# Attention stage of a hybrid layer: score tiles in a ring of three banks, q and k held twice, sample caches in the merge tile, attention written ahead of all projections

## The chip, the cores and the metric

One core of a Trainium2 chip runs the whole program in one launch. The time is device microseconds of that core. The kernel before took 1383.82, 1389.14 and 1391.13 us in three runs, so the median is 1389.14. The profile is of one more execution.

## The reference, cut to what matters

One layer of a streaming encoder runs on 512 prompt tokens and 32 sample tokens (the sample has a cache of 512 past keys and values). An input projection makes q, k and v of eight heads, the operands of a recurrent branch (RWKV-7) and two gates. Branch A is differential attention, the stage that changes: two softmax maps per head, subtracted with a learned factor, times v, then a norm per head.

```python
def diff_attend(q, k, v, lam, mask):          # q, k: 8 heads x 2 maps x 64; v: 8 heads x 128
    s = jnp.einsum('bqhcd,bkhcd->bchqk', q, k) * (DA_HEAD_DIM ** -0.5)
    if mask is not None:                      # the prompt: chunks of 64, block causal
        s = jnp.where(mask, s, -1e30)
    p = jax.nn.softmax(s, axis=-1)
    pd = p[:, 0] - lam * p[:, 1]
    return jnp.einsum('bhqk,bkhd->bqhd', pd, v)
...
x = x + (g_da * (o @ w_o_da) + g_rw * (o_rw @ w_o_rw)) @ w_out
x = x + ffn(rmsnorm(x))                       # up-projection, convolution of width 3, down-projection
```

## The kernel before, in words

Activations are held transposed, features on the 128 partitions and 544 tokens on the free axis (512 prompt, 32 sample). A projection (`dense_g`, L222) makes 128 output features in two halves of 272 tokens. Weights arrive in blocks of 128 x 512, a 256 KB load on SyncE's queue each (`load_w`, L212); ScalarE casts the high part `wh`, VectorE or GpSimd subtracts to get the low part `wl`, and a block gives 4 x 3 matmuls (`wh*xh`, `wh*xl`, `wl*xh`) for each half, 24 in all. One group of 1024 input features has two blocks, so 48 matmuls, into two tiles `psd` of PSUM, one for each half. Three `psd` banks exist. A half is evacuated when its last matmul is done.

The program has these stages: norm and recurrent branch with input projections among them; attention (L1091 to L1376), with what is left of the input projections ("fillers": v and gate tiles, written to DRAM by `fill_tile`) and the eight groups of `w_orw` among it; then the eight groups of `w_oda` (L1391), `w_out`, the up-projection, the down-projection and the last norm.

In the attention stage, `load_head` (L1252) fetches one head: v into `vt`; q and k into `raw`, split into `hi` (ScalarE) and `lo` (VectorE), and copied by small transfers into `Q`, `KH` and `KL`, so that both maps have all 128 partitions. Every one of these tiles has one buffer. `scores` (L1278) does a block of 128 queries: for each of the two maps a matmul with KH and one with KL into the tile `sc` (two banks, one buffer), a mask, a row maximum over both maps (`nm`, VectorE), two exponentials (`E`, ScalarE), and the difference `pd` (VectorE). `weighted` (L1308) transposes `pd`, copies it to `pdt`, and multiplies with v into `po`; after the fourth block `attend_norm` (L1113) makes the norm, and `finish_head` transposes back and writes `dh` and `dl` by `put_z`. `attend_sample` (L1177) does the same for four heads of the sample at once, against the caches in the tile `kc` (one buffer, first keys, then values).

The order around the change comes from two things. The program text is written by small generators that `Flow.run` interleaves by estimated due times (`yield ...`), with dense work in between. Then a scheduler builds each engine's queue: of the instructions whose operands and buffers it estimates to be ready, it takes the one written first. Each engine runs its queue in that order and waits at an instruction whose operand is late. SyncE's queue carries nearly all loads, also in order.

Of the kernel before, what the change touches and what calls it, by code (L numbers as in the profile page):

```python
# [10 lines left out]
F32 = mybir.dt.float32  # L11
F32R = mybir.dt.float32r
# [14 lines left out]
SEQ = 512  # L27
# [134 lines left out]
def tile_hybrid_layer(  # L162
# [931 lines left out]
    ap = ph2.enter_context(tc.tile_pool(name="ap", bufs=1, reuse_waits="tile"))  # L1094
    pst = ph2.enter_context(tc.tile_pool(name="pst", bufs=2, space=PSUM))
# [17 lines left out]
    def attend_norm(po, rz0, n, name="on"):  # L1113

        ssq = ap.tile([128, 4], F32, name="ssq", bufs=2)
        on = ap.tile([128, n, 128], F32, name=name)
# [19 lines left out]
    mg = mp.tile([128, KT, TOK], F32, name="mg")  # L1136
# [7 lines left out]

    zs = new_hl()
    load_z(mp, z_d, *zs, G)
    under = list(range(KT))
    flow.mark("z", 14.0)

    def orw_g(i):  # L1150
        nc.sync.dma_start(out=mg[:, i, :], in_=t_d[8 + i])

        def ev(ps, c0, c1):
            V.scalar_tensor_tensor(out=mg[:, i, c0:c1], in0=mg[:, i, c0:c1], scalar=1.0, in1=ps,
                                   op0=ALU.add, op1=ALU.mult)
        yield from dense_g(w_orw[i], KT, *zs, ev, V if i + 40 in FV else G)

    def choose2():
        if fillers:
            return fillers.pop(0)()  # L1160
        return orw_g(under.pop(0)) if under and flow.done["z"] <= PE.now else None

    att_dense = Dense(choose2)
# [9 lines left out]
    def load_caches(g):  # L1173
        caches[g] = ap.tile([128, 4, PAST], F32, name="kc")
        nc.sync.dma_start(out=caches[g], in_=kcache[4 * g:4 * g + 4].rearrange("a p t -> p a t"))

    def attend_sample(g):  # L1177
# [6 lines left out]
        yield PE.now + 1.0  # L1184
        sc = pssc.tile([128, 2, 512], F32, name="sc")
        kc = caches[g]
        for e, hh in enumerate(hs):
            for m in range(2):
                PE.matmul(sc[32 * e:32 * e + 32, m, :], qks[m * 64:m * 64 + 64, 0, hh, :],
                          kc[m * 64:m * 64 + 64, e, :], start=True, stop=True,  # L1190
                          tile_position=(64 * m, 32 * e))
        vc = ap.tile([128, 4, PAST], F32, name="kc").rearrange("p a (b v) -> p a b v", v=128)
        nc.sync.dma_start(out=vc, in_=vcache[4 * g:4 * g + 4].rearrange("a p b v -> p a b v"))
# [8 lines left out]
        V.tensor_reduce(out=nm, in_=sc, axis=AX.X, op=ALU.max, negate=True)  # L1202
        for m in range(2):
            V.tensor_reduce(out=nm2[:, m:m + 1], in_=scn[m][:, 0:32], axis=AX.X, op=ALU.max, negate=True)
        V.tensor_tensor(out=nm, in0=nm, in1=nm2, op=ALU.min)
        E = ap.tile([128, 2, 512], F32, name="E", bufs=2)
        En = ap.tile([128, 2, 32], F32, name="En")
        Z4 = ap.tile([128, 2, 2], F32, name="Z4")
        for m in range(2):
            A.activation(out=E[:, m, 0:PAST], in_=sc[:, m, :], func=AF.Exp, bias=nm[:, m:m + 1], scale=1.0,  # L1210
                         accum_out=Z4[:, 0, m:m + 1])
            A.activation(out=En[:, m, :], in_=scn[m][:, 0:32], func=AF.Exp, bias=nm[:, m:m + 1], scale=1.0,
                         accum_out=Z4[:, 1, m:m + 1])
# [21 lines left out]
        yield PE.now + 1.5  # L1235
# [8 lines left out]
        on = attend_norm(po[:, 0:1, :], rz1[:, 0:1], 1, "son")  # L1244
        yield PE.now + 5.0
# [32 lines left out]
    def scores(i, Q, KH, KL, rz):  # L1278

        nk = 128 * (i + 1)  # L1280
        sc = pssc.tile([128, 2, 512], F32, name="sc")
        nm = ap.tile([128, 2], F32, name="nm", bufs=3)
        E = ap.tile([128, 2, 512], F32, name="E", bufs=2)
# [3 lines left out]
        n = max(nk, 256)  # L1287
        for m in range(2):
            PE.matmul(sc[:, m, 0:n], Q[:, m, qb], KH[:, m, 0:n], start=True, stop=False)
            PE.matmul(sc[:, m, 0:n], Q[:, m, qb], KL[:, m, 0:n], start=False, stop=True)  # L1290
        V.memset(sc[0:64, :, nk - 64:nk], -1e30)
        V.tensor_reduce(out=nm, in_=sc[:, :, 0:nk], axis=AX.X, op=ALU.max, negate=True)
        for m in range(2):
            A.activation(out=E[:, m, 0:nk], in_=sc[:, m, 0:nk], func=AF.Exp, bias=nm[:, m:m + 1], scale=1.0,  # L1294
                         accum_out=Z[:, m:m + 1])
# [4 lines left out]
        V.scalar_tensor_tensor(out=pd[:, 0:nk], in0=E[:, 1, 0:nk], scalar=Z[:, 2:3], in1=E[:, 0, 0:nk],  # L1300
# [3 lines left out]
    def attention():  # L1304
# [3 lines left out]
        def weighted(h, i, pd, at, vtok, rz):  # L1308

            yield at  # L1310
# [9 lines left out]
            yield t  # L1320
# [11 lines left out]
        def finish_head():  # L1332
            yield last["at"]
# [8 lines left out]
        yield PE.now + 9.0  # L1342
        for h in range(HEADS):
# [5 lines left out]
            for i in range(4):  # L1349
                yield sc_free  # L1350
# [12 lines left out]
    def samples():  # L1363
        for g, h in ((0, 1), (1, 4)):
# [11 lines left out]
    hscope.close()  # L1376

# [279 lines left out]
```

## Time and profile before

| what | value |
|---|---|
| median of 3 runs | 1389.14 us (1383.82 to 1391.13) |
| profiled execution, its own time | 1387.72 us |
| its span, first to last instruction | 1385.9 us |
| TensorE busy | 1273.7 us, 92% |
| VectorE, ScalarE, GpSimd busy | 63%, 42%, 17% |
| mean granted TensorE clock | 0.941 of full speed |
| DMA | 185.9 MB, mean 134 GB/s |

The span is cut into 40 slices on the page; each digit is a busy share in tenths. A timeline names an instruction by line, engine and tiles (`out<-in`), with the idle time before it and what ended that. A granted clock of 1.00 is 2.4 GHz and 0.50 is 1.2 GHz; a mean between them is a mix of both.

### The profile page before, as it was taken

How to read it: one execution, taken by the hardware profiler on the slowest of the kernel's cores; microseconds unless marked ns; L12 is line 12 of the kernel's file. 1: busy time of each engine (PE TensorE's matmuls, PEld its weight loads, DVE VectorE, ACT ScalarE, POOL GpSimd, SP SyncE). 2: the span in 40 equal slices, each digit the busy share in tenths (PEclk: the TensorE clock that was granted, in tenths of full speed). 3: DMA queues.
4: the chain of work that ended last, by engine and by line, in shares of the span. 5: the costliest groups of instructions: out<-in, count | busy, mean ns of one | idle time of the engine just before them, and what ended most of it. 6: DMA issues, size and time to landing. Idle time of an engine off the chain costs nothing.

```text
span 1385.9 us, 29732 instructions
## 1 busy us (share of the span) xinstructions
PE 1273.7 (92%) x12014; PEld 1209.4 (87%) x12014; DVE 866.9 (63%) x1708; ACT 577.0 (42%) x1168; POOL 229.7 (17%) x264
## 2 busy tenths in 40 slices
PE   7799999799998999998899966699999999999996
PEld 7798898698877899988798944699999999999996
DVE  6867559765788234752466755566777888773333
ACT  5565544455312333323455543334444444443220
POOL 6500102112212102223212000000111111111111
PEclk9899888899989899999899987899999999999999
DMA  4254564154785353427776552245222222234321
GB/s 171 76 161 151 172 186 142 63 154 139 216 248 150 106 149 119 159 88 218 215 223 185 147 136 70 79 148 173 93 92 85 91 86 91 85 109 141 106 78 65
DMA packets 140330, 185.90 MB, mean 134 GB/s; under 512 B 42016, under 2 KB 65184, under 8 KB 140192
## 3 DMA queue, kind: packets, MB, share of 16 engines
q1 hardware_dynamic: 127120, 162.73, 39.4%
q10 hardware_dynamic: 13072, 21.26, 4.6%
q8 instruction: 95, 1.56, 0.5%
q14 instruction: 43, 0.35, 0.1%
HBM read 133.67 MB, written 37.41 MB: 123 GB/s over the span
## 4 chain that ended last, share of the span: by engine, by line
PE 76%; DVE 12%; ACT 4%; DMA 4%; issue 3%; SPq 1%; POOL 1%; DVEq 0%; ACTq 0%; POOLq 0%
PE psd L88 60%; PE misc L88 5%; PE psq L88 3%; PE psy L88 2%; PE sc L88 2%; PE misc L92 2%; PE po L88 1%; PE tp L92 1%; DVE NP L675 1%; ACT E L1294 1%; DVE XT L680 1%; DMA arL<-ar_d 1%; DMA t_d<-qt 1%; DMA bk_d<-bk 0%; DVE cs L526 0%
## 5 line engine op out<-in xcount | busy, mean ns | idle before, releaser
L218 ACT CAST wh<-wr 128x512 fp32r<-128x512 f32 (+1 forms) x316 | 192.4, 615 | 371.3 <-PE psd L88 314.0
L88 PE MATMUL psd<-h_h,wh 128*128 128x272 f32 x976 | 301.3, 309 | 5.5 <-ACT wh L218 5.4
L88 PE MATMUL psd<-h_l,wh 128*128 128x272 f32 x976 | 295.1, 302 | 0.2 <-DVE h_l L443 0.2
L88 PE MATMUL psd<-h_h,wl 128*128 128x272 f32 x976 | 293.3, 302 | 2.1 <-POOL wl L219 1.8
L219 DVE TENSOR_TENSOR wl<-wr,wh 128x512 fp32r<-128x512 f32 x230 | 158.6, 694 | 103.8 <-ACT wh L218 98.7
L88 PEld LDWEIGHTS psd<-h_h,wh 128*128 128x128 f32 x976 | 194.9, 200 | 11.3 <-ACT wh L218 6.3
L88 PE MATMUL psd<-xgh,wl 128*128 128x272 f32 x704 | 203.9, 290 | 0.0
L88 PE MATMUL psd<-xgl,wh 128*128 128x272 f32 x704 | 203.4, 289 | 0.0
L88 PE MATMUL psd<-xgh,wh 128*128 128x272 f32 x704 | 202.1, 287 | 0.0
L88 PEld LDWEIGHTS psd<-h_h,wl 128*128 128x128 f32 x976 | 193.5, 199 | 5.1 <-POOL wl L219 2.6
L88 PEld LDWEIGHTS psd<-h_l,wh 128*128 128x128 f32 x976 | 195.0, 200 | 3.2 <-issue 1.6
L219 POOL TENSOR_TENSOR wl<-wr,wh 128x512 fp32r<-128x512 f32 x86 | 120.5, 1406 | 384.4 <-ACT wh L218 333.8
L88 PEld LDWEIGHTS psd<-xgl,wh 128*128 128x128 f32 x704 | 132.6, 188 | 0.0
L88 PEld LDWEIGHTS psd<-xgh,wl 128*128 128x128 f32 x704 | 132.4, 188 | 0.0
L88 PEld LDWEIGHTS psd<-xgh,wh 128*128 128x128 f32 x704 | 132.1, 188 | 0.1
L88 PE MATMUL psd<-ah,wh 128*128 128x272 f32 x352 | 101.7, 289 | 0.0
L88 PE MATMUL psd<-ah,wl 128*128 128x272 f32 x352 | 101.5, 288 | 0.0
L88 PE MATMUL psd<-al,wh 128*128 128x272 f32 x352 | 101.4, 288 | 0.0
L88 PE MATMUL psd<-mh,wh 128*128 128x272 f32 x256 | 74.3, 290 | 0.0
L88 PE MATMUL psd<-mh,wl 128*128 128x272 f32 x256 | 74.3, 290 | 0.0
L88 PE MATMUL psd<-ml,wh 128*128 128x272 f32 x256 | 74.2, 290 | 0.0
L1455 POOL COPY cvo<-uf 128x2 f32<-128x2 f32 x88 | 37.2, 454 | 220.4 <-DVE uf L1452 220.4
(369 smaller groups left out, 2548.3 us busy)
## 6 DMA issues: line engine op xcount, KB each, us to landing
wr<-w_in SPq DMA_DIRECT2D x132, 256.0 KB, 3.1
wr<-w_up SPq DMA_DIRECT2D x88, 256.0 KB, 2.8
wr<-w_down SPq DMA_DIRECT2D x40, 256.0 KB, 2.7
bkL<-bk_d SPq DMA_DIRECT2D x16, 512.0 KB, 5.0
ar_d<-ar SPq DMA_DIRECT2D x8, 544.0 KB, 3.1
t_d<-qt ACTq DMA_DIRECT2D x16, 272.0 KB, 2.2
bk_d<-bk SPq DMA_DIRECT2D x32, 128.0 KB, 3.2
arL<-ar_d SPq DMA_DIRECT2D x8, 512.0 KB, 4.6
```

What stands on the lines that cost most here:

```text
L88: ins = self.pe.matmul(out, lhsT, rhs, **kw)
L92: ins = self.pe.transpose(out, in_, ident)
L218: A.copy(out=wh[:, :n], in_=raw)
L219: le.tensor_tensor(out=wl[:, :n], in0=raw, in1=wh[:, :n].bitcast(F32), op=ALU.subtract)
L675: V.transpose(out=npf[r0:r0 + 32, 0:1024], in_=mt[r0:r0 + 32, h, :, 32 * b:32 * b + 32].rearrange("p m t -> p t m"))
L680: V.transpose(out=XT[r0:r0 + 32, :, 32 * b:32 * b + 32].rearrange("p m i -> p i m"), in_=Xp[r0:r0 + 32].rearrange("p a i -> p i a"))
L1294: A.activation(out=E[:, m, 0:nk], in_=sc[:, m, 0:nk], func=AF.Exp, bias=nm[:, m:m + 1], scale=1.0, accum_out=Z[:, m:m + 1])
L1455: G.tensor_copy(out=cvo[:, t, :, w], in_=u[:, 512 + w::32])
```

## The change

All of it is in the attention stage.

- Scores: `sc` becomes a ring of three tiles of one bank. Blocks 0 and 1 (up to 256 keys) put both maps into one tile; blocks 2 and 3 take one tile for each map, with a mask and a maximum each. `E` becomes three tiles of one map.
- Loads: `Q`, `KH`, `KL` have two buffers; `raw` and `hi` still one; `lo` is written into `raw`; `vt` has 512 tokens.
- Caches: keys and values of a group of four heads are loaded together, ahead of the group, into the tile `mg`, which later holds the results of the `w_orw` groups. It has one buffer: the second group of caches waits for the first, and the `w_orw` results wait for the second.
- PSUM: the projections have two `psd` banks in this stage, not three; before the `w_oda` groups the pool is closed and opened again with three.
- Order: attention and samples are written first, with no due times, then all remaining fillers, then the loads of z and the `w_orw` groups. The scheduler alone puts projections among the heads. The samples follow heads 0 and 2, not 1 and 4.

```diff
     ap = ph2.enter_context(tc.tile_pool(name="ap", bufs=1, reuse_waits="tile"))
+    psd_scope[0].close()
+    psd_scope[0] = ExitStack()
+    psd[0] = psd_scope[0].enter_context(tc.tile_pool(name="psd", bufs=2, space=PSUM, side="right"))
...
-    mg = mp.tile([128, KT, TOK], F32, name="mg")
...
     def load_caches(g):
-        caches[g] = ap.tile([128, 4, PAST], F32, name="kc")
-        nc.sync.dma_start(out=caches[g], in_=kcache[4 * g:4 * g + 4].rearrange("a p t -> p a t"))
+        c = mp.tile([128, KT, TOK], F32, name="mg").rearrange("p a t -> p (a t)")
+        caches[g] = c[:, 0:4 * PAST].rearrange("p (a t) -> p a t", t=PAST), \
+            c[:, 4 * PAST:8 * PAST].rearrange("p (a b v) -> p a b v", b=4, v=128)
+        nc.sync.dma_start(out=caches[g][0], in_=kcache[4 * g:4 * g + 4].rearrange("a p t -> p a t"))
+        nc.sync.dma_start(out=caches[g][1], in_=vcache[4 * g:4 * g + 4].rearrange("a p b v -> p a b v"))
...
-        vt = ap.tile([128, TOK], F32, name="vt")
-        nc.sync.dma_start(out=vt, in_=v_d[h])
-        x = {n: ap.tile([128, 2, SEQ], F32R, name=n) for n in ("Q", "KH", "KL")}
+        vt = ap.tile([128, SEQ], F32, name="vt")
+        nc.sync.dma_start(out=vt, in_=v_d[h, :, 0:SEQ])
+        x = {n: ap.tile([128, 2, SEQ], F32R, name=n, bufs=2) for n in ("Q", "KH", "KL")}
...
-            raw = ap.tile([128, SEQ], F32, name="raw")
-            nc.sync.dma_start(out=raw, in_=d[h, :, 0:SEQ])
-            hi, lo = [ap.tile([128, SEQ], F32R, name=n) for n in ("hi", "lo")]
-            A.copy(out=hi, in_=raw)
-            V.tensor_tensor(out=lo, in0=raw, in1=hi.bitcast(F32), op=ALU.subtract)
+            raw = ap.tile([128, SEQ], F32R, name="raw")
+            nc.sync.dma_start(out=raw.bitcast(F32), in_=d[h, :, 0:SEQ])
+            hi = ap.tile([128, SEQ], F32R, name="hi")
+            A.copy(out=hi, in_=raw.bitcast(F32))
+            lo = raw
+            V.tensor_tensor(out=lo, in0=raw.bitcast(F32), in1=hi.bitcast(F32), op=ALU.subtract)
...
-        sc = pssc.tile([128, 2, 512], F32, name="sc")
...
-        E = ap.tile([128, 2, 512], F32, name="E", bufs=2)
...
+        if n == 256:
+            t = pssc.tile([128, 512], F32, name="sc", bufs=3).rearrange("p (m k) -> p m k", m=2)
+            sc = [t[:, m, :] for m in range(2)]
+        else:
+            sc = [pssc.tile([128, 512], F32, name="sc", bufs=3) for _ in range(2)]
+        E = [ap.tile([128, 512], F32, name="E", bufs=3) for _ in range(2)]
         for m in range(2):
-            PE.matmul(sc[:, m, 0:n], Q[:, m, qb], KH[:, m, 0:n], start=True, stop=False)
-            PE.matmul(sc[:, m, 0:n], Q[:, m, qb], KL[:, m, 0:n], start=False, stop=True)
-        V.memset(sc[0:64, :, nk - 64:nk], -1e30)
-        V.tensor_reduce(out=nm, in_=sc[:, :, 0:nk], axis=AX.X, op=ALU.max, negate=True)
+            PE.matmul(sc[m][:, 0:n], Q[:, m, qb], KH[:, m, 0:n], start=True, stop=False)
+            PE.matmul(sc[m][:, 0:n], Q[:, m, qb], KL[:, m, 0:n], start=False, stop=True)
+        if n == 256:
+            V.memset(t[0:64, :, nk - 64:nk], -1e30)
+            V.tensor_reduce(out=nm, in_=t[:, :, 0:nk], axis=AX.X, op=ALU.max, negate=True)
         for m in range(2):
+            if n > 256:
+                V.memset(sc[m][0:64, nk - 64:nk], -1e30)
+                V.tensor_reduce(out=nm[:, m:m + 1], in_=sc[m][:, 0:nk], axis=AX.X, op=ALU.max, negate=True)
...
-            yield at
+            yield PE.now
...
-        for g, h in ((0, 1), (1, 4)):
+        for g, h in ((0, 0), (1, 2)):
             load_caches(g)
             yield ("head", h), 0.0
             yield from attend_sample(g)
 
-    flow.run([attention(), samples()], att_dense)
-    att_dense.finish()
-    while att_dense.step():
-        att_dense.finish()
+    flow.run([samples(), attention()], Dense(lambda: None))
+    flow.mark("z", -1.0)
+    for f in fillers:
+        for _ in f():
+            pass
+    zs = new_hl()
+    mg = mp.tile([128, KT, TOK], F32, name="mg")
+    load_z(mp, z_d, *zs, G)
...
+    for i in range(KT):
+        for _ in orw_g(i):
+            pass
...
+    psd_scope[0].close()
+    psd_scope[0] = ExitStack()
+    psd[0] = psd_scope[0].enter_context(tc.tile_pool(name="psd", bufs=3, space=PSUM, side="right"))
```

How the queues stand now is read from the built programs. Line numbers in these rows are those of each kernel; `psd` is a projection, `tp` a transpose or another short result, `_d` a tensor in DRAM.

SyncE's queue at the start of the stage, before: `pd` first holds the lambda row, which stands just ahead of these rows, and `zr` is the recurrent branch's z.

```order
L1129 DMA zr_7810<-z_d_70 128x544
L1167 DMA qks_7842<-q_d_66 128x8x32
L1167 DMA qks_7842<-k_d_69 128x8x32
L1169 DMA vsc_7845<-v_d_67 128x8x32
L1255 DMA vt_7847<-v_d_67 128x544
L1129 DMA zr_7814<-z_d_70 128x544
L1260 DMA raw_7852<-q_d_66 128x512
L1175 DMA kc_7876<-kcache 128x4x512
L1129 DMA zr_7818<-z_d_70 128x544
L1267 DMA Q_7849<-hi_7854 64x512
L1267 DMA Q_7849<-lo_7855 64x512
```

The same place in the changed kernel, also from the row behind the lambda row on:

```order
L1149 DMA qks_7811<-q_d_66 128x8x32
L1149 DMA qks_7811<-k_d_69 128x8x32
L1151 DMA vsc_7814<-v_d_67 128x8x32
L1159 DMA mg_7816<-kcache 128x4x512
L1160 DMA mg_7816<-vcache 128x4x512
L1238 DMA vt_7819<-v_d_67 128x512
L1243 DMA raw_7824<-q_d_66 128x512
L217 DMA wr_9625<-w_in 128x512
L217 DMA wr_9661<-w_in 128x512
L217 DMA wr_9691<-w_in 128x512
L1238 DMA vt_7846<-v_d_67 128x512
```

Both caches of sample group 0 (1 MB each) now go ahead of the first `vt` and `raw`; z has gone from the place, and three weight loads (`wr`) stand in it.

TensorE before, at head 7, the last one (`sc_9980` is block 0, `sc_10052` block 1, `sc_10137` block 2):

```order
L88 MATMUL po_9871<-vtok_9720,pdt_10016 128x128 x4
L88 MATMUL sc_9980<-KH_9694,Q_9693 128x256
L88 MATMUL sc_9980<-KL_9695,Q_9693 128x256
...
L88 MATMUL sc_10052<-KH_9694,Q_9693 128x256
L88 MATMUL sc_10052<-KL_9695,Q_9693 128x256
...
L92 MATMUL tp_10068<-cst_92,pd_9994 128x128
L92 MATMUL tp_10130<-cst_92,on_10032 128x128 x4
L88 MATMUL po_10113<-vtok_9972,pdt_10070 128x128
L88 MATMUL psd_10480<-dh_7806,wh_10513 128x272
```

TensorE in the changed kernel, at the start of head 6 (`sc_9077`, `sc_9126` and the first half of block 2, `sc_9156`):

```order
L88 MATMUL sc_9077<-KH_8873,Q_8872 128x256
L88 MATMUL sc_9126<-KH_8873,Q_8872 128x256
L88 MATMUL sc_9156<-KH_8873,Q_8872 128x384
L88 MATMUL psd_10412<-ml_9987,wh_10415 128x272
L88 MATMUL psd_10412<-mh_9986,wl_10414 128x272
L88 MATMUL psd_10412<-mh_9986,wh_10415 128x272
...
L88 MATMUL sc_9077<-KL_8874,Q_8872 128x256
L88 MATMUL sc_9126<-KL_8874,Q_8872 128x256
L88 MATMUL sc_9156<-KL_8874,Q_8872 128x384
```

And at head 7:

```order
L88 MATMUL sc_9220<-KH_9043,Q_9042 128x256
L88 MATMUL sc_9269<-KH_9043,Q_9042 128x256
L88 MATMUL sc_9299<-KH_9043,Q_9042 128x384
L88 MATMUL sc_9220<-KL_9044,Q_9042 128x256
L88 MATMUL sc_9269<-KL_9044,Q_9042 128x256
L88 MATMUL sc_9299<-KL_9044,Q_9042 128x384
L88 MATMUL sc_9220<-KH_9043,Q_9042 128x256
L88 MATMUL sc_9269<-KH_9043,Q_9042 128x256
...
L88 MATMUL sc_9300<-KH_9043,Q_9042 128x384
L88 MATMUL sc_9300<-KL_9044,Q_9042 128x384
```

Before, three heads had only a few `w_oda` matmuls between their blocks. Now head 6 has `w_orw` matmuls between KH, KL and the second map, head 7 has no projection between its instructions, and three blocks begin before the first is finished.

TensorE in the changed kernel where sample group 1 reads its values (`tp_8522<-mg_8117`), in head 3 (`Q_8257`):

```order
L88 MATMUL sc_8616<-KH_8258,Q_8257 128x256
L88 MATMUL sc_8567<-KL_8259,Q_8257 128x256
L88 MATMUL sc_8616<-KL_8259,Q_8257 128x256
L88 MATMUL tp_8522<-mg_8117,pdt_8516 32x128 x16
L88 MATMUL tp_8522<-vs_8460,pdtn_8520 32x128 x4
...
L88 MATMUL sc_8674<-KH_8258,Q_8257 128x512
L88 MATMUL sc_8674<-KL_8259,Q_8257 128x512
L88 MATMUL psd_10087<-mh_9986,wh_10090 128x272
L92 MATMUL tp_8561<-cst_92,on_8544 128x128
```

SyncE in the changed kernel behind the load of head 3's keys (`KH_8258`):

```order
L1251 DMA KH_8258<-hi_8271 64x512 x2
L1251 DMA KL_8259<-raw_8269 64x512 x2
L1372 DMA mg_9988<-t_d_68 128x544 x2
L1243 DMA raw_8430<-q_d_66 128x512
L1372 DMA mg_9988<-t_d_68 128x544 x3
L1251 DMA Q_8427<-hi_8432 64x512
L1251 DMA Q_8427<-raw_8430 64x512
```

Between the last scores of head 2 and `psd_10087`, the second `w_orw` group, TensorE has no projection, and the loads of the gates into `mg_9988` stand ahead of head 4's `raw_8430` in SyncE's queue.

## Rows read from the trace of the kernel before

**Rows 1.** The page, busy tenths of TensorE in 40 equal slices.

```profile
PE   7799999799998999998899966699999999999996
```

**Rows 2.** Windows: us, busy us (xinstructions) by engine, TensorE clock, DMA share, GB/s.

```profile
639.00:700.00 61.00, 49.15 (x334) 46.76 (x335) 20.91 (x44) 26.66 (x68) 18.55 (x15) 0.89 0.75 233
700.00:800.00 100.00, 98.56 (x806) 91.63 (x806) 67.81 (x181) 54.64 (x159) 13.72 (x10) 1.00 0.63 181
800.00:883.00 83.00, 47.40 (x259) 35.14 (x257) 43.44 (x140) 33.16 (x115) 0.00 (x0) 0.74 0.32 84
890.00:930.00 40.00, 40.00 (x321) 40.00 (x320) 25.22 (x54) 13.65 (x27) 0.00 (x0) 1.00 0.46 137
```

**Rows 3.** Windows of the projection tile psd alone, same columns.

```profile
639.00:883.00 244.00, 123.54 (x799) 110.44 (x799) 6.95 (x16) 6.22 (x16) 0.88 0.56 161
...
700.00:800.00 100.00, 72.86 (x492) 64.85 (x492) 6.95 (x16) 1.58 (x4) 1.00 0.63 181
800.00:883.00 83.00, 7.90 (x35) 5.70 (x33) 0.00 (x0) 0.00 (x0) 0.74 0.32 84
```

**Rows 4.** Timeline of TensorE: start, us, instruction, idle before it and releaser.

```profile
639.01 0.63 PE L92 MATMUL tp<-cst,vt 128*128 128x128 f32 x4 [0.63 <-DMA vt<-v_d]
...
656.08 0.60 PE L88 MATMUL psd<-h_h,wh 128*128 128x272 f32 x1 [5.42 <-ACT wh L218]
...
661.45 0.41 PE L88 MATMUL sc<-KH,Q 128*128 128x256 f32 x1
...
750.65 0.36 PE L88 MATMUL sc<-KH,Q 128*128 128x256 f32 x1
...
775.33 0.28 PE L88 MATMUL sc<-KH,Q 128*128 128x256 f32 x1
```

**Rows 5.** Waits of TensorE, 800 to 883 us: total, times, longest.

```profile
PE sc L88 <- ACT E L1294: 4.4, 3, 2.6
PE sc L88 <- DMA KL<-lo: 4.3, 6, 1.0
```

**Rows 6.** Timeline of SyncE's queue in the last head's load.

```profile
849.24 1.10 SPq L1267 DMA_DIRECT2D KH<-hi  x2
...
852.96 1.24 SPq L1267 DMA_DIRECT2D KL<-lo  x2
```

**Rows 7.** Chain that ended last, 800 to 884 us: start, us, what.

```profile
843.82 1.21 PE sc L88 x4
...
867.07 1.21 PE sc L88 x4
...
883.08 1.05 PE psd L88 x3
```

**Rows 8.** DMA issues, median us to landing: 630 to 700, then 700 to 883.

```profile
Q<-hi SPq DMA_DIRECT2D x4, 128.0 KB, 4.1
...
KL<-lo SPq DMA_DIRECT2D x24, 128.0 KB, 2.3
...
Q<-lo SPq DMA_DIRECT2D x12, 128.0 KB, 2.4
...
raw<-q_d SPq DMA_DIRECT2D x5, 256.0 KB, 3.0
mg<-t_d SPq DMA_DIRECT2D x4, 272.0 KB, 3.9
```

**Rows 9.** Instructions, ns min/median/max; lo in 700 to 800, 800 to 883.

```profile
L1263 DVE TENSOR_TENSOR lo<-raw,hi x8: 683/690/1362, 699.7 to 796.4; 128x512 fp32r<-128x512 f32 x8
...
L1263 DVE TENSOR_TENSOR lo<-raw,hi x4: 682/693/693, 805.6 to 849.3; 128x512 fp32r<-128x512 f32 x4
...
L1262 ACT CAST hi<-raw x9: 614/618/633, 746.3 to 848.6; 128x512 fp32r<-128x512 f32 x9
...
L1292 DVE TENSOR_REDUCE nm<-sc x32: 424/822/1225, 666.8 to 868.6; 128x2 f32<-128x256 f32 x8, 128x2 f32<-128x512 f32 x8, 128x2 f32<-128x768 f32 x8, 128x2 f32<-128x1024 f32 x8
...
L1154 DVE SCALAR_TENSOR_TENSOR mg<-mg,psd 128x272 f32<-128x272 f32 x16 | 6.9, 434 | 7.2 <-PE psd L88 7.2
```

More of the change, by code (lines that the diff above doesn't have):

```diff
@@ L1111, in tile_hybrid_layer, with attend_norm @@
     fpool[0] = ap
-    def attend_norm(po, rz0, n, name="on"):
+    def attend_norm(po, rz0, n):
         ssq = ap.tile([128, 4], F32, name="ssq", bufs=2)
-        on = ap.tile([128, n, 128], F32, name=name)
+        on = ap.tile([128, 4, 128], F32, name="on")
         for i in range(n):
@@ L1143, in put_z @@
                                op0=ALU.mult, op1=ALU.subtract)
[L1145 to L1163, printed above, removed]
     qks = ap.tile([128, 2, HEADS, DEC], F32, name="qks")
@@ L1183, in attend_sample @@
         A.copy(out=vs, in_=ps[0:32].rearrange("p (e v) -> p e v", e=4))
-        yield PE.now + 1.0
-        sc = pssc.tile([128, 2, 512], F32, name="sc")
-        kc = caches[g]
+        yield PE.now
+        sc = [pssc.tile([128, 512], F32, name="sc", bufs=3) for _ in range(2)]
+        kc, vc = caches[g]
         for e, hh in enumerate(hs):
             for m in range(2):
-                PE.matmul(sc[32 * e:32 * e + 32, m, :], qks[m * 64:m * 64 + 64, 0, hh, :],
+                PE.matmul(sc[m][32 * e:32 * e + 32, :], qks[m * 64:m * 64 + 64, 0, hh, :],
                           kc[m * 64:m * 64 + 64, e, :], start=True, stop=True,
                           tile_position=(64 * m, 32 * e))
-        vc = ap.tile([128, 4, PAST], F32, name="kc").rearrange("p a (b v) -> p a b v", v=128)
-        nc.sync.dma_start(out=vc, in_=vcache[4 * g:4 * g + 4].rearrange("a p b v -> p a b v"))
         scn = [misc() for _ in range(2)]
@@ L1209, in attend_sample @@
         for m in range(2):
-            A.activation(out=E[:, m, 0:PAST], in_=sc[:, m, :], func=AF.Exp, bias=nm[:, m:m + 1], scale=1.0,
+            A.activation(out=E[m], in_=sc[m], func=AF.Exp, bias=nm[:, m:m + 1], scale=1.0,
                          accum_out=Z4[:, 0, m:m + 1])
@@ L1221, in attend_sample @@
         pdn = ap.tile([128, 32], F32, name="pdn")
-        V.scalar_tensor_tensor(out=pd, in0=E[:, 1, 0:PAST], scalar=Z[:, 2:3], in1=E[:, 0, 0:PAST], op0=ALU.mult, op1=ALU.add)
+        V.scalar_tensor_tensor(out=pd, in0=E[1], scalar=Z[:, 2:3], in1=E[0], op0=ALU.mult, op1=ALU.add)
         V.scalar_tensor_tensor(out=pdn, in0=En[:, 1, :], scalar=Z[:, 2:3], in1=En[:, 0, :],
                                op0=ALU.mult, op1=ALU.add)
-        yield PE.now + 5.5
+        yield PE.now
         ps = misc()
@@ L1234, in attend_sample @@
         A.copy(out=pdtn, in_=ps[0:32, 0:128])
-        yield PE.now + 1.5
+        yield PE.now
         po = misc().rearrange("p (a v) -> p a v", a=4)
@@ L1243, in attend_sample @@
             PE.matmul(po[q, 0, :], pdtn[:, q], vs[:, e, :], start=False, stop=True, tile_position=(0, 32 * e))
-        on = attend_norm(po[:, 0:1, :], rz1[:, 0:1], 1, "son")
-        yield PE.now + 5.0
+        on = attend_norm(po[:, 0:1, :], rz1[:, 0:1], 1)
+        yield PE.now
         ps = misc()
@@ L1299, in scores @@
         pd = ap.tile([128, 512], F32, name="pd", bufs=2)
[L1300 removed]
+        V.scalar_tensor_tensor(out=pd[:, 0:nk], in0=E[1][:, 0:nk], scalar=Z[:, 2:3], in1=E[0][:, 0:nk],
                                op0=ALU.mult, op1=ALU.add)
@@ L1308, in weighted @@
         def weighted(h, i, pd, at, vtok, rz):
-            yield at
+            yield PE.now
             ps = misc()
@@ L1319, in weighted @@
                 last["po"] = None
-            yield t
+            yield PE.now
             if i == 0:
@@ L1332, in finish_head @@
         def finish_head():
-            yield last["at"]
+            yield PE.now
             ps = misc()
@@ L1341, in attention @@
         nxt = load_head(0)
-        yield PE.now + 9.0
+        yield PE.now
         for h in range(HEADS):
@@ L1349, in attention @@
             for i in range(4):
-                yield sc_free
+                yield PE.now
                 pd = scores(i, Q, KH, KL, rz)
@@ L1367, in samples, with orw_g, ev @@
             yield from attend_sample(g)
-    flow.run([attention(), samples()], att_dense)
-    att_dense.finish()
-    while att_dense.step():
-        att_dense.finish()
+    flow.run([samples(), attention()], Dense(lambda: None))
[6 more added lines that the diff above has]
+    load_z(mp, z_d, *zs, G)
+    def orw_g(i):
+        nc.sync.dma_start(out=mg[:, i, :], in_=t_d[8 + i])
+        def ev(ps, c0, c1):
+            V.scalar_tensor_tensor(out=mg[:, i, c0:c1], in0=mg[:, i, c0:c1], scalar=1.0, in1=ps,
+                                   op0=ALU.add, op1=ALU.mult)
+        yield from dense_g(w_orw[i], KT, *zs, ev, V if i + 40 in FV else G)
+    for i in range(KT):
+        for _ in orw_g(i):
+            pass
     PE.pinned = False
```

8 lines of the change are left out of this document (4 added, 4 removed).

## The prediction

> **What bounds the kernel now.** I began with the page's busy row by slices [rows 1]: the reader is to see TensorE at seven tenths or more, and mostly nine, save a hole of three slices at six past the middle (and the last slice). The hole is the end of the attention stage, so I read that stage in windows [rows 2]. TensorE is busy for 98.6 of 100 us in the middle part at full clock, 49.2 of 61 before it, and only 47.4 of 83 behind it, there at a mean granted clock of 0.74. VectorE is at 68% in the full part and never above. The kernel is bound by TensorE with one hole in it, and the change works on the stage that holds the hole.
>
> How much is lost there? The stage runs from the first transposes of v, at 639.01, to the first matmul of the next stage behind attention, at 883.08 [rows 4, 7]: 244.1 us. In it stand 799 projection matmuls [rows 3]. At full clock one takes 0.125 us (321 in 40 us [rows 2]), so 99.9 us. A head's own TensorE work I take from a period without a gap: from the first score of head 3 at 750.65 to that of head 4 at 775.33 [rows 4] are 24.68 us, and the order has 131 projection matmuls in between (16.4 us), so a head is 8.3 us, eight are 66.4. A sample group is about 4 us (an estimate: of the 98.6 us 492 projections are 61.5 [rows 3], and some four heads leave about this), two are 8. That makes 174.3 us of work in 244.1: 69.8 us are idle or at half clock.
>
> Why? The waits of the hole [rows 5] show a chain inside one head: scores wait for the exponentials that still hold the one score tile, 4.4 us, and for KL that is still landing, 4.3; other links of the chain wait in the same way. Nothing stands in the queue to cover them, because the projections have run out: 35 of 799 lie behind 800 us [rows 3].
>
> **What the change does, part by part.** Work on TensorE is the same but for place. From the same instruction on (the two orders agree up to the row before the first transposes of v in the old kernel) the new order has 736 projection matmuls to the end of attention, not 799; 63 of the o_da group go behind it, 63 x 0.125 = 7.9 us back. The 736 are spread as 148 ahead of the first score, then 100, 104, 48, 55, 82, 104 and 95 in the periods that begin with heads 0 to 6, and none in head 7. So seven heads have cover where four and a half had it.
>
> What paces a head is now its load chain, since Q, KH and KL have two buffers but raw and hi have one, and the low part is written into raw. k's raw therefore waits until q's parts have landed, and the next q until KL has. From rows: raw 3.0, hi 0.62, lo 0.69, two more issues of 0.6, landing 2.4; raw 3.0 again, hi 0.62, from the first KH issue to the last KL issue 4.4 (849.24 to 853.6), landing 2.3 [rows 6, 8, 9]. The sum is 18.2 us. Beside projections the old chain was longer too: a period took 24.68 with them and 23.25 in the bare tail (843.82 to 867.07 [rows 4, 7]), so I add 1.4. The bounds are 18.2 and 26: in the busy start q's parts took 4.1 to land, not 2.4 [rows 8], and if every landing is as slow the sum is 25; one more wait on SyncE's queue makes 26. I take 21, near the sum.
>
> The row of lo has 0.69 as its median and 1.36 as its longest while POOL works, and 0.69 at most in the window in which POOL has no instruction [rows 2, 9]. The Trainium skill, page "SBUF — State Buffer", section "SBUF: two separate sides", says that GpSimd and a VectorE instruction with two SBUF inputs lock each other out of a shared port for a whole instruction. By that rule both lo of each head would sit on the chain at 1.36, 1.3 us more a head and 9 us in all; the trace agrees for single ones, and my sum goes without it.
>
> The pieces, each the larger of its TensorE work and the chain:
> - first transposes to first score: 148 x 0.125 + 0.6 = 19.1; the 2 MB of caches go ahead of the first raw, so I take 21. Before it was 22.4 (661.45 [rows 4]) for 109, with a wait of 5.4 for a weight cast [rows 4], whose load stood on SyncE's queue behind a row of q, k and z transfers. The new queue has three weight loads where the old has none, so I count that wait as gone.
> - head 0 with sample group 0: 12.5 + 8.3 + 4 = 24.8
> - head 1: 13.0 + 8.3 = 21.3; head 5 the same 21.3
> - heads 2, 3, 4: work of 16.3, 17.2 (each with half a sample group), 18.6; the chain decides, 21 each. The o_rw groups can't go on here: their result tile is the tile that holds the caches, so group 0's two banks stay full until group 1 of the samples has read its v, t_d has landed (3.9 [rows 8]) and VectorE has evacuated (0.43 [rows 9]). In the order this falls at the head of the period of head 3.
> - head 6: 11.9 + 8.3 = 20.2, so 21
> - head 7 with no cover: now 883.08 less 855.9 (last KL issued at 853.6 and 2.3 to land) = 27.2, of which 11.2 before the scores of block 3 (867.07). Those 11.2 shrink with three banks, since a block needn't wait for the exponentials of the one before. I put them between 5 and 11, and take 7: 23.
> - stalls that the order doesn't foresee: the first 61 us had 11.9 idle [rows 2], 6.5 of it not the weight cast; I carry 8.
>
> Sum: 21 + 24.8 + 21.3 + 3 x 21 + 21.3 + 21 + 23 + 8 = 203.4. Against 244.1 that is 40.7 less, 7.9 come back behind: 32.8 us. The profiled execution took 1387.72 (span 1385.9 and 1.8 around it), 1.4 under the median of the runs, 1389.14, and inside their spread. 1387.7 - 32.8 is 1354.9; I say 1356.
>
> **Costed at nothing.** VectorE gets two more reduces and two more memsets a head. From 256 to 1024 elements the reduce goes from 0.424 to 1.225, so its fixed part is 0.16 us, and the memset is not likely dearer: 0.64 a head. VectorE's 68% hides it; without cover it would be 5 us. The shorter vt and the two tiles for E move no time. Two added waits stand on SyncE's in-order queue: the second kcache load waits for the last matmul that reads sample group 0's v, and the first t_d load for the same of group 1. Behind them stand the next head's raw, its Q parts and the o_rw weights, and TensorE waits for these. In the order both come when the next raw would not be free earlier, so nothing to a few us, inside the 8.
>
> **Rivals.**
> - *The load chain is slower, 23.5 a head.* Then heads 1 to 6 are 141 and head 0 is 24.8, the sum 218: 18 us gained, 1369. For it: in-place lo, three single buffers in a row, weight loads between them on the same queue. Against it: the old order kept TensorE full for 100 us although its chain was tight there too.
> - *Nothing gained.* At 26 a head the sum is 234 and the gain 2: 1386. This needs every landing as slow as in the busy start.
> - *Slower: two projection banks instead of three.* A half of a group must be evacuated while the other half runs its last 12 matmuls, 1.5 us; later than that TensorE stands still. With 736 matmuls there are 31 halves, so the gain is eaten when each comes 1.05 us past that cover, and at 2 us past it the time is 1387.7 - 32.8 + 62 = 1417; at 1.3 it is 1395. For it: VectorE and ScalarE run their queues in order, with exponentials and reduces that wait in front. Against it: VectorE was idle for 7.2 us before the 16 evacuations, waiting for TensorE [rows 9], so it came early. The Trainium skill, page "Perfetto Trace Analysis", section "Optimizing Tensor Performance", wants matmul groups to rotate through banks so that one's evacuation lies under the next; two banks leave that only by halves. No run here has two banks yet.
>
> **How the numbers follow.** Forecast 0.57, with its own range 1345 to 1366 (chain 18.2 to 22.5, the last head 21 to 27, stalls 2 to 12); the slower chain 0.24; nothing gained 0.10; slower 0.09. A measurement of this kernel can't tell under about 0.5% (7 us) from no change. The forecast and the slower chain are faster: 0.81. The range holds 1342 to 1384: it leaves out the slower rival and part of the third, and below only a stage with hardly a stall.
>
> **What would show it.** In the new profile the hole should be one head long, some 23 us. The first wait for a weight cast should be gone. The first KH scores of heads 1 to 6 should stand 21 us apart, and next raw should be issued right as KL has landed. TensorE should show one stretch with little projection work near heads 2 to 4, ended by VectorE's first write to mg. If the distances are 24 or more, with TensorE waiting for KL, the second case holds. If projection matmuls wait for an evacuation at many half groups, the last one does. I am wrong altogether if TensorE is idle for more than 50 us between the first transposes of v and the o_da group.

## The result, and the profile after

| kernel | median, us (lowest to highest, runs) | ratio to before, 95% interval |
|---|---|---|
| before, beside it | 1386.51 (1383.82 to 1391.13, 4) | 1 |
| changed | 1365.65 (1363.36 to 1372.14, 4) | 0.9854 [0.9805, 0.9903] |
| changed, once more | 1362.43 (1359.57 to 1364.22, 6) | 0.9819 [0.9792, 0.9845] |

The change gains 20.9 us in the first comparison and 26.4 in the second, where 32.8 were forecast (1356 us). In the second the kernel before beside it has a median of 1388.86 (17 runs); over all comparisons its medians go from 1386.3 to 1388.9, so the ratios are the fairer measure between two of them. Below, "the mark" is the second comparison, since most experiments were timed in as many rounds. It was expected at 1362 to 1370 with the same waits in its trace, and came so.

The profiled execution took 1367.84 us, its span is 1366.0. Its busy row of TensorE and the granted clock, which answer to [rows 1]:

```profile
PE   8798998799989899999987997999999999999996
...
PEclk9899898899989899999998998999999999999998
```

The hole of three slices at six is gone; left are an 8 and a 7 (683 to 751 us) and a 7 further on (820 to 854), each slice 34.15 us long. Windows of the changed kernel from the first score of each head to that of the next (the last one ends at the first w_oda matmul), with the columns of [rows 2]:

```profile
661.63:686.42 24.79, 24.30 (x174) 19.00 (x175) 13.85 (x36) 13.81 (x41) 2.69 (x2) 1.00 0.78 221
686.42:718.75 32.33, 27.47 (x217) 25.47 (x215) 19.16 (x62) 18.91 (x54) 8.25 (x6) 0.90 0.71 205
718.75:741.14 22.39, 16.56 (x130) 12.87 (x130) 16.13 (x50) 13.15 (x43) 3.90 (x3) 0.96 0.61 172
741.14:767.10 25.96, 20.86 (x150) 18.05 (x150) 15.95 (x60) 11.65 (x38) 3.08 (x2) 0.77 0.65 187
767.10:789.35 22.25, 21.02 (x157) 19.16 (x155) 13.44 (x43) 13.08 (x41) 3.86 (x3) 1.00 0.55 149
789.35:812.39 23.04, 21.10 (x161) 19.95 (x159) 16.23 (x51) 13.69 (x44) 2.91 (x3) 1.00 0.61 168
812.39:831.81 19.42, 19.42 (x150) 18.76 (x150) 14.54 (x43) 10.57 (x30) 0.95 (x1) 1.00 0.56 149
831.81:855.93 24.12, 12.59 (x56) 9.21 (x55) 13.93 (x53) 9.59 (x36) 0.00 (x0) 0.71 0.22 62
```

Read the first number behind the window as the head's period. Six of eight lie between 19.4 and 24.8. Head 1 (the second row, 32.3) and head 3 (the fourth, 26.0 at a mean clock of 0.77) stand out, and head 7 is as uncovered as before. The timeline of TensorE at these places, which answers to [rows 4, 7]:

```profile
640.22 0.39 PE L88 MATMUL psd<-h_h,wh 128*128 128x272 f32 x1 [2.41 <-ACT qt L888]
...
657.81 0.39 PE L88 MATMUL psd<-h_h,wh 128*128 128x272 f32 x1 [1.82 <-ACT qt L888]
...
701.65 1.66 PE L88 MATMUL po<-vtok,pdt 128*128 128x128 f32 x8 [2.18 <-ACT pdt L1308]
...
741.14 0.58 PE L88 MATMUL sc<-KH,Q 128*128 128x256 f32 x1 [3.36 <-DMA KH<-hi]
...
749.19 0.44 PE L88 MATMUL sc<-KH,Q 128*128 128x384 f32 x1 [1.75 <-ACT E L1287]
...
752.22 0.79 PE L88 MATMUL sc<-KH,Q 128*128 128x512 f32 x1 [2.41 <-ACT E L1287]
...
855.20 1.09 PE L92 MATMUL tp<-cst,on 128*128 128x128 f32 x4 [4.79 <-DVE on L1125]
```

The wait of 5.42 for a weight cast [rows 4] is gone. New are two waits for `qt`, the tile into which a filler's projection is evacuated, and waits for ScalarE's copy `pdt` in head 1 (two, of 2.18 and 2.02). The longest waits of TensorE, 644 to 860 us, as [rows 5] has them for its stretch:

```profile
PE sc L88 <- DMA KH<-hi: 6.1, 4, 3.4
PE sc L88 <- ACT E L1287: 6.0, 4, 2.4
PE po L88 <- ACT pdt L1308: 5.8, 5, 2.2
PE tp L92 <- DVE on L1125: 4.8, 1, 4.8
```

The cause of those for `pdt` stands in two other queues. SyncE's queue of the changed kernel at the head of that period:

```profile
684.91 1.23 SPq L1251 DMA_DIRECT2D KL<-raw  x2
690.05 0.33 SPq L1132 DMA_DIRECT2D zr<-z_d  x1
691.01 0.63 SPq L1159 DMA_DIRECT2D mg<-kcache  x1
691.74 0.51 SPq L1243 DMA_DIRECT2D raw<-q_d  x1
692.31 0.42 SPq L1160 DMA_DIRECT2D mg<-vcache  x1
700.87 0.47 SPq L1251 DMA_DIRECT2D Q<-hi  x1
```

Then what the `zr` load waited for (SyncE's waits, 686 to 720 us), how long that one `raw` took to land, what all DMA queues moved in that time (691.74 to 700.23 us), and ScalarE's timeline behind it:

```profile
SPq L1132 <- POOL ml L1134: 6.9, 2, 3.8
```

```profile
DMA to landing us min/median/max: 8.5/8.5/8.5
```

```profile
DMA packets 1274, 2.50 MB, mean 295 GB/s; under 512 B 64, under 2 KB 64, under 8 KB 1274
```

```profile
700.23 0.62 ACT L1245 CAST hi<-raw 128x512 fp32r<-128x512 f32 x1 [2.38 <-DMA raw<-q_d]
...
701.02 0.58 ACT L1308 COPY pdt<-tp 128x512 f32<-128x512 f32 x1
...
712.97 0.40 ACT L888 ACTIVATE qt<-psd 128x272 f32<-128x272 f32 x1 [2.06 <-DMA t_d<-qt]
713.26 0.61 ACT L1245 CAST hi<-raw 128x512 fp32r<-128x512 f32 x1
...
714.29 0.48 ACT L1308 COPY pdt<-tp 128x384 f32<-128x384 f32 x1
```

Three delays can be read off. SyncE reached `raw` at 691.74; the last KL issue (the second of the pair at 684.91) began at 685.6, and a landing is 2.3 from its issue [rows 8], so the tile was free at 687.9 and 3.9 us were lost, most behind the `zr` load at 690.05, which waited 3.8 for GpSimd. Then `raw` stood between 1 MB of keys, issued 0.7 us ahead, and 1 MB of values, issued 0.6 behind, and landed in 8.5 us, not 3.0 [rows 8]: 5.5 more. The values took part in that: of the 2.50 MB moved in those 8.5 us, the keys, `raw`, `zr` and the `qt` on its way to DRAM are 1.9 at most, which leaves at least 0.6. Then ScalarE waited 2.06 at 712.97, until the single `qt` was emptied to DRAM, with the cast of k's `hi` and a `pdt` queued behind. Together 11.5 us, and the period is 32.3 where 21.3 were forecast; nc1 below says how much of it hangs on the caches.

### The profile page after: what moved, and what is told of

It reads as the page before. It is cut to its first block, busy times and chain, and to the rows that moved or that the text cites. A ratio compares the mean times of both kernels' runs of the same rounds, so it can differ in the third digit from the quotient of the medians.

```text
span 1366.0 us, 29766 instructions
## 1 busy us (share of the span) xinstructions
PE 1264.7 (93%) x12014; PEld 1201.0 (88%) x12014; DVE 860.2 (63%) x1742; ACT 575.9 (42%) x1168; POOL 229.1 (17%) x264
```

## The experiments

All kernels are the changed one with the edit shown.

**nc1, no caches of its own for sample group 1**.

```diff
-            load_caches(g)
+            if g:
+                caches[g] = caches[0]
+            else:
+                load_caches(g)
```

> The second sample group computes with the first group's caches, so its own 2 MB are not loaded; the rest of the changed kernel stands. Theory (the gain is missing at single places, the largest in the period that begins with head 1): the raw of q of head 2 took 8.5 us to land there, behind the first of these megabytes, where the others take about 3.0; without it that period falls from 32.3 to about 26, and the time from 1365.6 to about 1360. Rival 1 (the load chain is slow in every head): the period falls by 2 at most and the time stays within 2 us of 1365.6. Rival 2 (the cover is only moved): the period falls, but later heads have fewer projections beside them and give it back, and the time stays above 1363.

Measured: 1363.68 us, 0.9846 [0.9819, 0.9874]. Windows from first score to first score, heads 1, 2 and 3:

```profile
686.42:711.42 25.00, 22.63 (x198) 20.43 (x196) 19.34 (x61) 16.68 (x50) 8.26 (x6) 1.00 0.59 168
711.42:736.27 24.85, 22.44 (x150) 16.22 (x149) 14.09 (x44) 13.72 (x40) 4.11 (x3) 0.86 0.54 160
736.27:764.95 28.68, 20.61 (x152) 17.25 (x144) 16.37 (x63) 12.26 (x43) 2.97 (x2) 0.76 0.68 185
```

The period of head 1 fell from 32.3 to 25.0, so 7.3 of the 11.0 us over the forecast hang on the caches: that `raw` landed in 4.5 us, and ScalarE's wait for `qt` is gone too. (The edit takes away both megabytes, so it doesn't tell the keys ahead of `raw` from the values behind it.) The wait of `zr` for GpSimd is still there, 3.7. But the time isn't apart from the mark: heads 2 and 3 went from 22.4 and 26.0 to 24.9 and 28.7, heads 6 and 7 from 19.4 and 24.1 to 21.1 and 25.7. The theory's period came, its time did not, and the second rival holds. What was gained in one head was lost again in later ones.

**qt2, two buffers for qt.** The space came from the sample's v, loaded into the free end of the cache tile (that part of the edit isn't shown).

```diff
-        qt = fpool[0].tile([128, TOK], F32, name="qt")
+        qt = fpool[0].tile([128, TOK], F32, name="qt", bufs=1 if fpool[0] is rp else 2)
...
```

> The evacuation tile qt has two buffers (the space comes from the sample's v, now in the free end of the cache tile). Theory: with two projection banks TensorE waits for evacuations into qt, and these wait for the DMA that empties the one qt; the three waits of TensorE ended by qt (0.5, 2.4 and 1.8 us) go, and with them ScalarE's wait of 2.1 in the period of head 1, behind which the copy pdt and the cast hi stood; 5 to 7 us, about 1360. Rival (the waits lie beside the load chain, which sets the end): the waits go, the distances of the heads' first scores stay within 1 us, and the time is 1364 to 1366.

Measured: 1360.74 us, 0.9809 [0.9784, 0.9834]. TensorE's waits for qt in the stage fell from 4.2 to one of 1.0 (the 0.5 stands ahead of the stage and stayed), head 1 to 29.3, and first score to first score of the other heads moved by up to 1.4. That is 1.7 us below the mark and 4.9 below the first run, with intervals that overlap: the waits are explained, their worth in time is not settled.

**p3, three projection banks, two score banks; sc2, two score banks alone.**

```diff
-    psd[0] = psd_scope[0].enter_context(tc.tile_pool(name="psd", bufs=2, space=PSUM, side="right"))
+    psd[0] = psd_scope[0].enter_context(tc.tile_pool(name="psd", bufs=3, space=PSUM, side="right"))
...
-            sc = [pssc.tile([128, 512], F32, name="sc", bufs=3) for _ in range(2)]
+            sc = [pssc.tile([128, 512], F32, name="sc", bufs=2) for _ in range(2)]
```

The score tile changes so at its three places; sc2 has that part alone.

> Three projection banks again and two score banks instead of three. Theory (the score ring is worth more than the third projection bank): TensorE no longer waits for qt (4.7 us less), but its waits for exponentials rise from 6 us to 15 or more, most in the head without cover; about 1369. Rival (two projection banks are the price of the change, and the third score bank brings little): 1358 to 1361.

> The changed kernel with two score banks instead of three and still two projection banks; one bank stays unused. Theory (the third score bank is worth little, so the gain of the form with three projection and two score banks is that of the projection banks alone): 1361 to 1367, 0.2 to 0.3% at most from the changed kernel, though the waits for exponentials grow by some us. Rival (the third score bank is worth 6 us or more, and the third projection bank that much more than the other form showed): 1369 to 1375.

Measured: p3 1353.72 us, 0.9769 [0.9747, 0.9790]; sc2 1362.64 us, 0.9834 [0.9807, 0.9861]. The theory for p3 was wrong (its waits for exponentials are 3.1 us, not 15), its rival right in kind, with a time 4 us under its range. sc2's time came as expected, but its waits for exponentials didn't grow. The two differ in one thing, the third projection bank, and their intervals are apart: that bank is worth 8.9 us by the medians (by the intervals, an estimate, 4 to 14). Waits of TensorE in sc2, 640 to 860 us:

```profile
PE sc L88 <- ACT E L1287: 4.0, 8, 1.2
PE psd L88 <- ACT qt L888: 4.0, 3, 2.1
```

and in p3 the waits for the same exponentials, 640 to 852 us, then the first w_oda matmul in p3 and in sc2:

```profile
PE sc L88 <- ACT E L1287: 3.1, 3, 2.3
```

```profile
814.04 0.29 PE L88 MATMUL psd<-dh,wh 128*128 128x272 f32 x1
```

```profile
830.85 0.39 PE L88 MATMUL psd<-dh,wh 128*128 128x272 f32 x1 [0.30 <-DVE mg L1375]
```

The changed kernel waits 6.0 for these exponentials with three score banks, so a third one doesn't lessen them in sum. The waits for qt are 4.0 in sc2 and 0.6 in p3. The profiled pair is closer than the medians: of its 6.1 us (spans of 1360.8 and 1354.7) 2.5 had arisen before the stage, where both run the same instructions, and 3.6 are left, about the 3.4 of those waits. What the rest of the 8.9 is, or whether it is noise, stays open.

It isn't w_oda: sc2 and p3 both have 63 w_oda matmuls ahead of attention's end, from 26 and 37 us before it on, while the changed kernel's first stands at that end, at 855.93. So two projection banks alone don't hold them back; in sc2, where one bank lies free, they go in. This also clouds what the third score bank is worth: sc2 gives up that bank and gains those matmuls, and its time is that of the mark. In the last head the bank does what it was meant to: from KL's last landing (issue and 2.3 us) to the first score of block 3 are 11.2 us before [rows 7], 7.5 in sc2 and 5.5 in the changed kernel.

**nore, two projection banks up to the end of the w_oda groups,** opened with three only behind them.

```diff
     hscope.close()
-    psd_scope[0].close()
-    psd_scope[0] = ExitStack()
-    psd[0] = psd_scope[0].enter_context(tc.tile_pool(name="psd", bufs=3, space=PSUM, side="right"))
...
     ms2.close()
+    psd_scope[0].close()
+    psd_scope[0] = ExitStack()
+    psd[0] = psd_scope[0].enter_context(tc.tile_pool(name="psd", bufs=3, space=PSUM, side="right"))
```

> The pool of projection banks stays at two banks through the w_oda groups and is opened with three behind them, so that w_oda matmuls may stand among the last heads: 42 do. Theory (two banks cost in two ways: TensorE's waits for qt, some 5 us, and the w_oda matmuls that the reopened pool holds back until attention's last bank is free): the second cost goes for 42 matmuls, 5 us, and the time is about 1360. Rival (the gain of the three-bank form is the waits for qt alone): 1364 to 1367, or more where the w_oda stage waits with two banks.

Measured: 1363.17 us, 0.9834 [0.9804, 0.9864], between theory and rival and inconclusive against the mark. w_oda began at 826.98, with 42 matmuls ahead of attention's end, so the mechanism is there, but the time can't show it. That letting w_oda in is worth something is not shown, here or by sc2.

**s1, sample group 1 behind head 1, not head 2.**

```diff
-        for g, h in ((0, 0), (1, 2)):
+        for g, h in ((0, 0), (1, 1)):
```

> The second sample group follows head 1, not head 2, so that the tile mg is free for the w_orw groups a head earlier. Theory (projections are cover that is only placed elsewhere): the stretch without projections at head 3 goes, with its waits of 3.4, 1.8 and 2.4 us, but the projections now run out a head earlier, heads 6 and 7 are both uncovered, and the time is 1364 to 1369. Rival (the stretch at head 3 is what the prediction missed): 1358 to 1361.

Measured: 1356.97 us, 0.9787 [0.9764, 0.9809]; a little below the rival's 1358 to 1361, so the rival holds against the theory. That it is faster than the mark (0.9792 to 0.9845) isn't quite shown: the intervals overlap a little. Head 3 of s1:

```profile
737.72:760.68 22.96, 21.79 (x163) 19.95 (x161) 13.38 (x43) 13.59 (x46) 3.16 (x3) 1.00 0.61 168
```

22.96 us at full clock, where the changed kernel has 25.96 at 0.77; head 1 is 27.7. Heads 6 and 7 are uncovered then, as the theory said, but an uncovered head 6 took 20.5 from first score to first score, little more than the 19.4 with 95 projections. Two limits lie close together there: the covered head 6 is TensorE's own work (busy for 19.42 of 19.42 us), while in the uncovered one TensorE is busy for 11.2 us and the loads of q into raw stand 20.4 apart (785.64 and 806.04), so there the load chain sets the distance.

**qk1, one buffer for Q, KH and KL; qk1p3, the same with three projection and two score banks.**

```diff
-        x = {n: ap.tile([128, 2, SEQ], F32R, name=n, bufs=2) for n in ("Q", "KH", "KL")}
+        x = {n: ap.tile([128, 2, SEQ], F32R, name=n) for n in ("Q", "KH", "KL")}
```

> One part undone: Q, KH and KL have one buffer again. Theory (the second buffers are the part that brings the gain, since a head's load no longer waits for the scores of the head before): the first scores of the heads stand 25 us or more apart, and the time is 1378 to 1390. Rival (order and cover make the gain, the load chain has slack): 1364 to 1370.

> Of the changed kernel neither the second buffers of Q, KH and KL nor the third score bank; three projection banks. What is left of the change is the order, the caches in mg and the low part in raw. Theory (the second buffers carry the gain): the chain is then 23 to 28 a head as in the run with one buffer, three banks give back some 8 us of it, and the time is 1370 to 1376. Rival (order and caches are a gain of their own of some 20 us, and two projection banks hid it): 1362 to 1367.

Measured: qk1 1381.54 us, 0.9963 [0.9943, 0.9982]; qk1p3 1385.02 us, 0.9974 [0.9955, 0.9993]. Waits of SyncE's queue in qk1, 640 to 868 us, and its last head on TensorE:

```profile
SPq L1251 <- PE sc L88: 26.5, 6, 8.2
```

```profile
841.50 1.08 PE L88 MATMUL sc<-KH,Q 128*128 128x256 f32 x3 [4.27 <-DMA KH<-hi]
```

SyncE stands 26.5 us with a copy into Q or KH that the scores of the head before still read, and the first scores are 23.6 to 30.6 apart (three of the seven distances under the expected 25). So nearly all of the gain needs the second buffers; the rest of the change brings 0.3 to 0.4% without them. For qk1p3 both expectations were wrong: three banks gave nothing back here. TensorE's waits for qt, 4.6 us in qk1, fell to 0.4, and 63 w_oda matmuls went ahead of attention's end, but the time didn't fall, as it would not where the load chain sets the end. What the second buffers would bring in the old order was not tried.

**raw2, two buffers for raw,** and the sample's v moved as in qt2 (not shown).

```diff
-            raw = ap.tile([128, SEQ], F32R, name="raw")
+            raw = ap.tile([128, SEQ], F32R, name="raw", bufs=2)
...
```

> raw has two buffers (the space comes from the sample's v, now in the free end of the cache tile), so that k's raw loads while q's parts are copied. The scheduler then puts 397 projections ahead of and among the heads, not 698. Theory (the load chain through the one raw paces heads 4 to 6, with 21.6 to 23.6 us from one raw of q to the next): these distances fall by 3 to 5, and the time is 1352 to 1362. Rival (in-order queues of ScalarE and SyncE pace them, whatever raw has): the distances stay above 21 with fewer projections beside them, and the time is 1375 or more.

Measured: 1354.94 us, 0.9781 [0.9757, 0.9805]. SyncE's queue of raw2, then its windows from the first score of heads 4, 5 and 6 to that of the next:

```profile
709.20 0.59 SPq L1243 DMA_DIRECT2D raw<-q_d  x1
713.00 0.37 SPq L1243 DMA_DIRECT2D raw<-k_d  x1
```

```profile
731.57:751.33 19.76, 13.85 (x63) 12.08 (x63) 12.81 (x41) 11.12 (x35) 3.06 (x3) 0.63 0.54 151
751.33:767.93 16.60, 12.42 (x67) 10.84 (x65) 12.50 (x40) 11.28 (x42) 2.86 (x2) 0.79 0.66 181
767.93:787.61 19.68, 17.21 (x93) 14.45 (x94) 15.73 (x53) 12.46 (x39) 2.91 (x2) 0.83 0.67 189
```

k's raw follows q's by 2 to 4 us. The first scores of heads 4 to 7 stand 19.8, 16.6 and 19.7 apart, with 7, 11 and 39 projections beside them, where the changed kernel has 22.3, 23.0 and 19.4, with 82, 104 and 95. From one raw of q to the next are 15.9, 26.1 and 17.5 us (changed: 23.0, 23.6 and 21.6), so the distances fell by 2.9 on average, not by 3 to 5 each. The time is in the theory's range and far from the rival's, though its interval just overlaps the mark's, and fewer projections beside the heads are part of the shorter distances. Two other readings bear the theory out. In the changed kernel three of the seven next loads of q into raw go out within 0.13 us of KL's landing. One of them, the last, behind the last pair of KL issues, whose second began at 812.40 and landed at 814.81:

```profile
811.76 1.24 SPq L1251 DMA_DIRECT2D KL<-raw  x2
...
814.93 0.33 SPq L1243 DMA_DIRECT2D raw<-q_d  x1
```

And the same second buffer, added to p3s1 below, gains clear of noise.

**p3s1 and raw2p3s1, edits together:** p3 with s1, then raw2 as well.

> Both edits that gained: three projection banks with two score banks, and the second sample group behind head 1. Theory (they fill different holes: the start and the last head by the one, head 3 by the other): the gains add, 12 and 8.7 us, about 1345. Rival (the same projections are cover in both): 1351 to 1354.

> The edits that gained, together: two buffers for raw, three projection banks with two score banks, the second sample group behind head 1. Theory (the load chain and the places of the projections are two limits, and each edit lifts another): 1340 to 1347. Rival (each fills the same holes, which are now bound by TensorE and by the exponentials): 1348 to 1354.

Measured: p3s1 1350.34 us, 0.9751 [0.9727, 0.9775], near the rival (and 0.7 below its range): the edits share most of their gain. raw2p3s1 1342.79 us, 0.9682 [0.9656, 0.9708], inside the theory's range and better than both kernels. The two differ in raw's second buffer (with the sample's v moved), which is worth 7.6 us here, their intervals apart. The TensorE row of raw2p3s1 on the page, with one 7 and one 8 left past the middle:

```profile
PE   8799998799999899999997899999999999999996
```

## Why the prediction came out as it did

The direction was right, and so was the load chain as the pace of the heads; the gain came out at 64% (20.9 of 32.8) in the first comparison, at the far end of the stated range, and 80% (26.4) in the second. Several terms were too small, and chance helped the profiled time. The forecast's pieces against the profiled execution and the profile of the repeat:

| piece | forecast | profiled | repeat |
|---|---|---|---|
| to the first score | 21 | 26.0 | 25.4 |
| head 0 | 24.8 | 24.8 | 24.4 |
| head 1 | 21.3 | 32.3 | 31.7 |
| head 2 | 21 | 22.4 | 22.1 |
| head 3 | 21 | 26.0 | 25.6 |
| head 4 | 21 | 22.3 | 22.0 |
| head 5 | 21.3 | 23.0 | 22.5 |
| head 6 | 21 | 19.4 | 19.4 |
| head 7 | 23 | 24.1 | 24.1 |
| unforeseen stalls | 8 | in the pieces | in the pieces |
| sum | 203.4 | 220.3 | 217.2 |

(The stage begins at the program row of [rows 4]'s first transposes, here at 635.64: the 38th projection ahead of the transposes of v.) So the stage shrank by 23.8 us, of which 7.3 came back behind it (forecast 7.9): 16.5, half of the forecast. The profiled spans differ by 19.9; the 3.4 that are left were there before the stage began, in code that the change doesn't touch. In the profiled runs with the same order of instructions up to there, that point lies between 632.7 and 639.0 us, so these 3.4 are luck.

- *To the first score, 21:* 26.0. Two projection banks were costed at nothing, and TensorE waits 4.2 us for qt here; p3 takes 22.2 (636.41 to 658.64) with a wait of 0.6.
- *Load chain, 21 a head:* right in kind, a little short. Heads 2, 4, 5 and 6 average 21.8, one raw of q to the next is 21.6 to 23.6 in the last three, and a second raw is worth 7.6 us (raw2p3s1 against p3s1). Head 6, at 19.4, is set by TensorE's work. The rival of 23.5 in every head would have given about the measured time by another way; the trace has two late heads, not eight.
- *Head 0 and head 7:* 24.8 is right. The 23 of head 7 came near (24.1) by two errors that cancel. It was counted from KL's last landing, the pieces ahead of it up to the first score, and the 3.7 us between the two (831.81 to 835.53) stood in no piece. From the landing on it is 20.4: the 11.2 us ahead of block 3 became 5.5, not 7. The third score bank is 2.0 of that (sc2 has 7.5); sc2 changes the rest of the score tiles as the changed kernel does.
- *Head 1 at 21.3:* the step that failed most, by 11.0. I costed the second caches' load on SyncE at a few us and only as a wait. The wait was 0.9; the two megabytes around raw's load made it 5.5 longer (nc1: the period is 7.3 shorter without them), and I had left out zr's wait for GpSimd in the same queue and qt's for its DMA.
- *Head 3 at 21:* I saw the stretch without projections, ended by the gates' loads, but took the chain as its length. Without cover the score blocks wait for exponentials one after the other (1.75 and 2.41), partly at half clock; s1 takes 3.0 us off this head, and its median is 5.5 below the mark's.
- *Two projection banks at no cost, and as a rival with 31 late halves:* both wrong in shape. The price exists, 8.9 us by the medians of sc2 and p3, but it isn't 1.3 us at each half. What the traces show of it is a few waits for the one qt behind the banks, 4.0 against 0.6 us; the rest is open. The Trainium skill, page "Perfetto Trace Analysis", section "Optimizing Tensor Performance", wants groups to rotate through banks; sc2 and p3 agree with it, at 8.9 us for the third bank.
- *lo at 0.69 on the chain:* right, though the prediction gave no reason for it. In the kernel before, five of the 16 met a GpSimd instruction already running and took 1.06 to 1.36 us. In the changed kernel 14 of 16 meet none, the other two began first, and none takes longer than 0.694:

```profile
L1247 DVE TENSOR_TENSOR raw<-raw,hi x16: 678/691/694, 646.4 to 829.3; 128x512 fp32r<-128x512 f32 x16
```

The lock that the Trainium skill describes (page "SBUF — State Buffer", section "SBUF: two separate sides") is seen elsewhere. The same instruction of the two sample groups, VectorE's timeline, with GpSimd in a subtraction from 687.10 to 688.72 and idle at the second:

```profile
687.51 1.26 DVE L1206 SCALAR_TENSOR_TENSOR pdn<-En,Z 128x32 f32<-128x32 f32 x1
...
741.67 0.25 DVE L1206 SCALAR_TENSOR_TENSOR pdn<-En,Z 128x32 f32<-128x32 f32 x1
```

```profile
687.10 1.62 POOL L219 TENSOR_TENSOR wl<-wr,wh 128x512 fp32r<-128x512 f32 x1 [7.34 <-ACT wh L218]
```

It ends at 688.77, right behind GpSimd, so the trace agrees; 1.0 us was lost there.

## What to carry to other kernels

When a second buffer lifts one wait, walk the whole chain behind it for the next single tile (here raw, then qt) and price every load on its queue by the bytes that are under way with it, not only by the wait. An edit that fills one hole (nc1, 7 us in head 1) can be worth nothing when later stretches lose as much, while the same work placed elsewhere (s1, 5.5 us by the medians) costs nothing to try. A pool that is closed and reopened can hold back what comes behind it where no bank is free (w_oda from 855.93 on, 830.85 with a free bank), but look whether lifting that shows in the time: nore and sc2 don't show it. A spare bank was worth more to the long stream of projections than to the scores (p3 against the mark, 8.7 us by the medians).

## What was not expected of the hardware

A load of 256 KB issued 0.7 us behind one of 1 MB and 0.6 us ahead of another on the same queue landed in 8.5 us, where the others of its size take about 3.0; without the two no transfer from or into raw took over 5.1 in nc1. Behind TensorE's wait of 4.79 us in the last head the first w_oda matmuls start 0.225 us apart, not 0.125, at a granted clock of 0.50 (1.2 GHz; 855.93 to 858 us), so work that comes back behind an uncovered head costs more than its price at full clock.
